# Unsplit expert tiles of a PEER layer over four PSUM banks instead of two, and 40 of them instead of 36

## The chip, the cores and the metric

The kernel runs on one core of one Trainium2 chip. The metric is the device time of one execution in microseconds (us). TensorE (PE) multiplies matrices and writes to PSUM, VectorE (DVE) and ScalarE (ACT) work elementwise, GpSimd (POOL) does so too and issues gathers from DRAM, and SyncE (SP) issues the plain loads and stores. Each engine takes its instructions strictly in the order in which they were written for it. "PEld" is the load of the stationary operand into TensorE.

## The reference

One layer for a prompt of 256 tokens and 8 samples of 16 tokens (128 tokens): modulated norm, a wide projection, an RWKV branch and a sparse attention branch, a mix of the two, and then PEER, a layer that picks experts by product keys. The change lies in PEER:

```python
def block(hb):                                   # 128 tokens, D = 1024
    q = (hb @ w_pq).reshape(PEER_BLOCK, PEER_HEADS, 2, PEER_DHALF)
    s = jnp.einsum('nhpd,hpkd->nhpk', q, peer_keys).astype(jnp.float32)
    s1, i1 = lax.top_k(s[:, :, 0], PEER_TOPK)
    s2, i2 = lax.top_k(s[:, :, 1], PEER_TOPK)
    cand = (s1[..., :, None] + s2[..., None, :]).reshape(PEER_BLOCK, PEER_HEADS, PEER_TOPK * PEER_TOPK)
    ...
    sc, j = lax.top_k(cand, PEER_TOPK)
    e = jnp.take_along_axis(cidx, j, axis=-1)
    g = jax.nn.softmax(sc, axis=-1)
    act = jax.nn.gelu(jnp.einsum('nhkd,nd->nhk', peer_u[e], hb).astype(jnp.float32))
    return jnp.einsum('nhk,nhkd->nd', (g * act).astype(hb.dtype), peer_v[e])
```

There are 8 heads, 16 picks for each and 16,384 experts, and all data is 32-bit floating point.

## The kernel before

Everything up to PEER takes the first half of the span. PEER treats the two groups of tokens in two ways.

- The 128 sample tokens go the sparse way (`peer_sparse`): for each of 128 picks, one gather by POOL brings a row of `peer_u` and `peer_v` for each token into a ring of three buffers (`raw`, L1573). DVE forms the dot product with the token (L1580), ACT applies gelu and the weight (L1581, L1582), and DVE adds the weighted row to `acc` (L1586). One such round is called a pull here. A gather waits until the `acc` of three pulls earlier has freed its buffer.
- The 256 prompt tokens go the dense way: all 16,384 experts are computed, as 128 u tiles of 128 experts (`dense_u`), the result is multiplied by a weight that is zero for experts not picked (`weights`), and 128 v tiles (`dense_v`) sum up the output.

A u tile loads 128 x 1024 numbers into one of four buffers `w`, multiplies them with the tokens into a PSUM tile of 128 x 256, and ACT writes the gelu of that to `G` (L1489), which frees the PSUM tile. The first `N1` u tiles are unsplit: 8 products of plain 32-bit operands with `h2f`, each of which the compiler turns into two matrix instructions, 16 for a tile. From tile `N1` on, a tile is split: ACT rounds it to a high part `wh` (L230), DVE subtracts for a low part `wl` (L234), and TensorE does 24 products with the split tokens `h2h` and `h2l`. So an unsplit tile asks nothing of DVE and one short gelu of ACT, and a split tile asks 128 x 1024 of each besides.

The unsplit tiles stand in the code beside the selection (`peer_select`, which finds the picks on DVE for the three groups of 128 tokens). After them the memory of `h2f` and of the selection is given up and taken over by the buffers of the split tiles and of `weights`: the first `wh` waits for the last read of `h2f`, and the first work of `weights` on DVE (L1424) waits for the last transposes of the selection's result `pix` on TensorE (L1384). Tiles `N1` to 75 follow, then `weights` with 31 more split u tiles among it, then the v tiles with the last 21 u tiles.

PSUM has eight banks, shared out by `PSB` under five names: `mm` 2 (projections, later `weights`), `fx` 2, `bx` 1, `dx` 2, `cp` 1. A u tile takes the name `u`, which stands for `fx`; so the u tiles go round two banks.

A pull is asked for after every u tile from tile `S0` = 30 on, at half a pull for each. But the order of the instructions of every engine is not the order of the code: a scheduler with a model of durations sets it, and moves pulls and u tiles forward to where it sees an engine free. No order is changed on the chip.

```python
PSB = {"mm": 2, "fx": 2, "bx": 1, "dx": 2, "cp": 1}
ALIAS = {"ix": "cp", "cs": "bx", "u": "fx"}
```

Of the kernel before, what the change touches and what calls it, by code (L numbers as in the profile page):

```python
# [176 lines left out]
ORDER = "GGIggggR1R23DMMMGRMRDMRGMGMRMDGMMRRMGDMMMGGGMGGM"  # L177


N1, NW, NA, NB = 36, 76, 8, 24  # L180
SR, UR = (0.5, 0.5, 0.62), 0.5
S0, PH = 30, 4
OFF = [j for j in range(NW, 128) if (j - NW + 1) * NB // (128 - NW) > (j - NW) * NB // (128 - NW)]
# [12 lines left out]
class K:  # L196
# [1274 lines left out]
    def dense_u(self, j):  # L1471

        nc = self.nc
        u = self.expert(self.I["puT"][j].rearrange("p k e -> p (k e)"))
        p = self.ps([128, 256], tag="u")
        if j < N1:
            u = u.rearrange("p (k e) -> p k e", k=8)
            for k in range(8):
                self.mm(p, u[:, k], self.h2f[:, k], start=(k == 0), stop=(k == 7))
        else:  # L1480
            uh, ul = (x.rearrange("p (k e) -> p k e", k=8) for x in self.split(u, UENG[j % len(UENG)]))
            hi, lo = self.h2p
            for k in range(8):
                self.mm(p, uh[:, k], hi[:, k], start=(k == 0), stop=False)
                self.mm(p, uh[:, k], lo[:, k], start=False, stop=False)
                self.mm(p, ul[:, k], hi[:, k], start=False, stop=(k == 7))
        off = j in OFF
        g = self.G[:, j] if j < NW else self.t([128, 256], tag="gO" if off else "gA", bufs=2 if off else NA, pool=self.late)
        nc.scalar.activation(g, p, AF.Gelu_apprx_tanh)  # L1489
        if off:  # L1490
            nc.sync.dma_start(self.Ad[OFF.index(j)], g)
        return g
# [262 lines left out]
```

## Time and profile before

| | us |
|---|---|
| median of three executions | 1782.42 |
| the three | 1770.41, 1782.42, 1785.15 |
| the profiled execution | 1775.45 |
| its span, first to last instruction | 1773.6 |
| mean granted TensorE clock in it | 0.977 of full speed |

All times below are from the profiled execution, counted from its first instruction. PEER's dense part has three stages there: the selection with the unsplit tiles beside it (some 880 to 1027), the split tiles and `weights` (1027 to 1300), and the v tiles (1300 to the end). A row of the timeline gives start, duration, engine, line, operation, the tile written and the tiles read, how many instructions were merged into the row, and in brackets the idle time before it and what ended that. Durations overlap on TensorE and, by a little, on DVE, so that what an instruction costs in a full queue is the distance from its start to the next start.

### The profile page before, as it was taken

How to read it: one execution, taken by the hardware profiler on the slowest of the kernel's cores; microseconds unless marked ns; L12 is line 12 of the kernel's file. 1: busy time of each engine (PE TensorE's matmuls, PEld its weight loads, DVE VectorE, ACT ScalarE, POOL GpSimd, SP SyncE). 2: the span in 40 equal slices, each digit the busy share in tenths (PEclk: the TensorE clock that was granted, in tenths of full speed). 3: DMA queues.
4: the chain of work that ended last, by engine and by line, in shares of the span. 5: the costliest groups of instructions: out<-in, count | busy, mean ns of one | idle time of the engine just before them, and what ended most of it. 6: DMA issues, size and time to landing. Idle time of an engine off the chain costs nothing. (4 is left out here: it accounts for less than half of the span.)

```text
span 1773.6 us, 33200 instructions
## 1 busy us (share of the span) xinstructions
PE 1682.0 (95%) x12424; PEld 1409.4 (79%) x12424; DVE 1358.9 (77%) x2911; ACT 751.1 (42%) x1670; POOL 537.9 (30%) x616
## 2 busy tenths in 40 slices
PE   6999899999999999999999989999999999999988
PEld 4888788777888877999878789999976667767766
DVE  4448778777867766556999998899847777778787
ACT  4533343334342333334323365577843433433344
POOL 2433243333333320034033222422233224223331
PEclk8999899999999999999999999999999999999999
DMA  8543662455365356755488989987569999999995
GB/s 307 156 125 98 184 192 70 144 166 168 94 205 149 101 198 188 247 188 187 129 336 320 370 310 383 378 316 261 178 236 362 347 349 379 354 364 385 340 366 218
DMA packets 172537, 436.71 MB, mean 246 GB/s; under 512 B 46036, under 2 KB 86100, under 8 KB 155992
## 3 DMA queue, kind: packets, MB, share of 16 engines
q1 hardware_dynamic: 153944, 300.36, 50.4%
q0 software_dynamic: 18432, 134.23, 19.8%
q8 instruction: 98, 1.61, 0.4%
q14 instruction: 63, 0.52, 0.1%
HBM read 403.23 MB, written 31.30 MB: 245 GB/s over the span
## 5 line engine op out<-in xcount | busy, mean ns | idle before, releaser
L234 DVE TENSOR_TENSOR wl<-w,wh 128x1024 fp32r<-128x1024 f32 (+1 forms) x280 | 351.1, 1261 | 106.7 <-ACT wh L230 69.8
L230 ACT ACTIVATE wh<-w 128x1024 fp32r<-128x1024 f32 (+1 forms) x288 | 300.3, 1051 | 162.0 <-PE mm L226 75.0
L1573 POOL DMA_INDIRECT raw<-in_puv,pe x128 | 172.8, 1350 | 430.1 <-PE dx L226 137.1
L226 PE MATMUL fx<-h2h,wh 128*128 128x256 f32 x736 | 210.6, 286 | 4.6 <-ACT wh L230 4.2
L226 PE MATMUL fx<-h2h,wl 128*128 128x256 f32 x736 | 208.3, 284 | 5.9 <-DVE wl L234 5.7
L226 PE MATMUL fx<-h2l,wh 128*128 128x256 f32 x736 | 206.5, 281 | 0.0
L1586 DVE SCALAR_TENSOR_TENSOR acc<-raw,dots,acc 128x1024 f32<-128x1024 f32 x127 | 167.4, 1318 | 15.1 <-ACT dots L1582 15.0
L1580 DVE SCALAR_TENSOR_TENSOR raw<-raw,sh 128x1024 f32<-128x1024 f32 x128 | 159.5, 1246 | 15.2 <-DMA raw<-in_puv,pe 15.1
L226 PEld LDWEIGHTS fx<-h2h,wh 128*128 128x128 f32 x736 | 139.6, 190 | 10.0 <-ACT wh L230 7.5
L226 PEld LDWEIGHTS fx<-h2h,wl 128*128 128x128 f32 x736 | 139.2, 189 | 9.0 <-DVE wl L234 8.3
L226 PEld LDWEIGHTS fx<-h2l,wh 128*128 128x128 f32 x736 | 139.7, 190 | 1.8 <-issue 1.4
L226 PE MATMUL fx<-h2f,w 128*128 128x256 f32 x576 | 129.5, 385 | 7.2 <-ACT G L1489 7.2
L226 PEld LDWEIGHTS fx<-h2f,w 128*128 128x128 f32 x576 | 109.4, 192 | 25.4 <-ACT G L1489 10.0
L226 PE MATMUL mm<-LTh,wh 128*128 128x384 f32 (+2 forms) x352 | 123.4, 351 | 1.8 <-ACT wh L230 1.0
L226 PE MATMUL mm<-LTl,wh 128*128 128x384 f32 (+2 forms) x352 | 123.0, 349 | 1.3 <-POOL LTl L488 1.3
L226 PE MATMUL mm<-LTh,wl 128*128 128x384 f32 (+2 forms) x352 | 122.3, 347 | 0.0
L226 PE MATMUL mm<-wh,LTh 128*128 128x256 f32 x336 | 100.4, 299 | 2.9 <-ACT qx L888 2.9
L226 PE MATMUL mm<-wl,LTh 128*128 128x256 f32 x336 | 99.6, 297 | 0.0
L226 PE MATMUL mm<-wh,LTl 128*128 128x256 f32 x336 | 98.9, 294 | 0.0
L1581 ACT ACTIVATE dots<-dots 128x1 f32<-128x1 f32 x128 | 25.6, 200 | 154.9 <-DVE raw L1580 154.4
L226 PEld LDWEIGHTS mm<-LTh,wh 128*128 128x128 f32 (+2 forms) x352 | 66.4, 189 | 7.6 <-issue 2.8
L226 PEld LDWEIGHTS mm<-wh,LTh 128*128 128x128 f32 x336 | 65.5, 195 | 5.5 <-ACT qx L888 3.1
(576 smaller groups left out, 4167.0 us busy)
## 6 DMA issues: line engine op xcount, KB each, us to landing
w<-in_puT SPq DMA_DIRECT2D x128, 512.0 KB
w<-in_pv SPq DMA_DIRECT2D x128, 512.0 KB
w<-in_w_in SPq DMA_DIRECT2D x70, 512.0 KB
w<-in_w_ada SPq DMA_DIRECT2D x48, 512.0 KB
cKT<-in_cKT SPq DMA_DIRECT2D x32, 256.0 KB
cV<-in_cV SPq DMA_DIRECT2D x32, 256.0 KB
w<-in_w_pq SPq DMA_DIRECT2D x16, 512.0 KB
d<-wst SPq DMA_DIRECT2D x8, 832.0 KB
```

What stands on the lines that cost most here:

```text
L226: return self.nc.tensor.matmul(out, l, r, start=start, stop=stop, skip_group_check=True, **kw)
L230: self.nc.scalar.activation(hi, src, AF.Copy)
L234: (self.nc.vector if eng == "v" else self.nc.gpsimd).tensor_tensor(lo, src, hi, op=OP.subtract)
L1573: d = nc.gpsimd.indirect_dma_start(out=bass.AP(tensor=u.tensor, offset=u.offset, ap=[u.ap[0], [1, 2048]]), out_offset=None, in_=self.I["puv"],
L1580: nc.vector.scalar_tensor_tensor(u, u, 1.0, h2, op0=OP.mult, op1=OP.mult, accum_out=dot)
L1581: nc.scalar.activation(dot, dot, AF.Gelu_apprx_tanh)
L1586: nc.vector.scalar_tensor_tensor(acc, v, dot, acc, op0=OP.mult, op1=OP.add)
```

## The change

```diff
-N1, NW, NA, NB = 36, 76, 8, 24
+N1, NW, NA, NB = 40, 76, 8, 24
@@ dense_u(self, j)
-        p = self.ps([128, 256], tag="u")
+        p = self.ps([128, 256], tag="mm" if j < N1 and j % 2 else "u")
```

Unsplit tiles with an odd number now go to the two `mm` banks, the others stay in the two `fx` banks, so that four banks hold u tiles while the selection runs; the split tiles keep two. Tiles 36 to 39 (counted from 0), which were split, become unsplit. Elsewhere the code is the same; the scheduler's order around the border of the two stages is not. Three places follow; in them `fx` and `mm` read from `h2f` are unsplit tiles, `fx` read from `h2h`, `h2l` are split ones, and the products of `oh` are those of `weights`.

TensorE at the border, before: the last two unsplit tiles, the three transposes of the selection's result (`dx`), and the first split tiles.

```order
L226 MATMUL fx_11740<-h2f_9800,w_11738 128x256 x8
L1384 MATMUL dx_11297<-cfirst,pix_11259 128x128
L226 MATMUL fx_11752<-h2f_9800,w_11750 128x256 x8
L1384 MATMUL dx_11297<-cfirst,pix_11259 128x128
L1384 MATMUL dx_11297<-cfirst,pg_2219_11290 128x128
L226 MATMUL fx_11783<-h2h_11769,wh_11784 128x256
L226 MATMUL fx_11783<-h2l_11770,wh_11784 128x256
L226 MATMUL fx_11815<-h2h_11769,wh_11816 128x256
L226 MATMUL fx_11815<-h2l_11770,wh_11816 128x256
L226 MATMUL fx_11783<-h2h_11769,wl_11785 128x256
```

TensorE at the same border in the changed kernel, from the 37th unsplit tile on.

```order
L226 MATMUL fx_11771<-h2f_9800,w_11769 128x256 x8
L226 MATMUL mm_11783<-h2f_9800,w_11781 128x256 x5
L1384 MATMUL dx_11297<-cfirst,pix_11259 128x128
L1384 MATMUL dx_11297<-cfirst,pg_2219_11290 128x128
L226 MATMUL mm_11783<-h2f_9800,w_11781 128x256 x3
L226 MATMUL fx_11802<-h2f_9800,w_11800 128x256 x8
L226 MATMUL mm_11814<-h2f_9800,w_11812 128x256 x8
L226 MATMUL mm_13141<-oh_13138 128x128 x4
L226 MATMUL bx_13155<-oh_13148 128x128 x4
L226 MATMUL mm_13207<-oh_13204 128x128 x4
L226 MATMUL fx_11845<-h2h_11831,wh_11846 128x256
L226 MATMUL fx_11845<-h2l_11832,wh_11846 128x256
```

The last transposes now stand inside the 38th unsplit tile, with 2 3/8 unsplit tiles behind them, and three groups of `weights` stand ahead of the first split tile.

DVE behind the last reduction of the selection (L1365), before: one `acc`, the first small work of `weights`, and the first `wl`.

```order
L1365 TENSOR_REDUCE pix_11259<-poh_11283 128x64
L1586 SCALAR_TENSOR_TENSOR acc_11699<-raw_13410,dots_13412,acc_11699 128x1024
L1424 CAST wA_13206<-pT_2172_11065 128x128
L1448 TENSOR_TENSOR oh_13218<-pT_2172_11065,dx_13204 128x512
L1425 TENSOR_SCALAR wA_13206<-wA_13206 128x128
L234 TENSOR_TENSOR wl_11785<-w_11781,wh_11784 128x1024
L1426 CAST wab_13207<-wA_13206 128x128
```

DVE at the same place in the changed kernel.

```order
L1365 TENSOR_REDUCE pix_11259<-poh_11283 128x64
L1586 SCALAR_TENSOR_TENSOR acc_11699<-raw_13330,dots_13332,acc_11699 128x1024
L1580 SCALAR_TENSOR_TENSOR raw_13397,dots_13399<-raw_13397,sh_2290_11697 128x1024
L1586 SCALAR_TENSOR_TENSOR acc_11699<-raw_13397,dots_13399,acc_11699 128x1024
L1424 CAST wA_13126<-pT_2172_11065 128x128
L1448 TENSOR_TENSOR oh_13138<-pT_2172_11065,dx_13124 128x512
L1425 TENSOR_SCALAR wA_13126<-wA_13126 128x128
L1426 CAST wab_13127<-wA_13126 128x128
L1580 SCALAR_TENSOR_TENSOR raw_13470,dots_13472<-raw_13470,sh_2290_11697 128x1024
```

A whole pull, the 27th, now stands ahead of `weights`, and no `wl`.

DVE a few rows on, before: the rows up to the `wl` of the 41st u tile (the fifth split one).

```order
L1580 SCALAR_TENSOR_TENSOR raw_13550,dots_13552<-raw_13550,sh_2290_11697 128x1024
L234 TENSOR_TENSOR wl_11888<-w_11884,wh_11887 128x1024
L1401 TENSOR_TENSOR oh_13218<-wA_13213,wB_13214 128x512
L1401 TENSOR_TENSOR oh_13228<-wA_13213,wB_13214 128x512
L1401 TENSOR_TENSOR oh_13284<-wA_13213,wB_13214 128x512
L1448 TENSOR_TENSOR oh_13284<-pT_2172_11065,dx_13204 128x512
L1580 SCALAR_TENSOR_TENSOR raw_13616,dots_13618<-raw_13616,sh_2290_11697 128x1024
L1586 SCALAR_TENSOR_TENSOR acc_11699<-raw_13550,dots_13552,acc_11699 128x1024
L234 TENSOR_TENSOR wl_11927<-w_11923,wh_11926 128x1024
```

DVE in the changed kernel, right behind the rows above: up to the `wl` of the 41st u tile (here the first split one).

```order
L1427 SCALAR_TENSOR_TENSOR wab_13127<-wab_13127,pT_2172_11065 128x128
L1437 TENSOR_TENSOR wA_13133<-wab_13127,clate 128x256
L1440 TENSOR_TENSOR wB_13134<-wab_13127,clate 128x512
L1439 TENSOR_TENSOR wA_13133<-wA_13133,pT_2172_11065 128x256
L1586 SCALAR_TENSOR_TENSOR acc_11699<-raw_13470,dots_13472,acc_11699 128x1024
L1401 TENSOR_TENSOR oh_13138<-wA_13133,wB_13134 128x512
L1401 TENSOR_TENSOR oh_13148<-wA_13133,wB_13134 128x512
L1401 TENSOR_TENSOR oh_13204<-wA_13133,wB_13134 128x512
L1448 TENSOR_TENSOR oh_13204<-pT_2172_11065,dx_13124 128x512
L1580 SCALAR_TENSOR_TENSOR raw_13536,dots_13538<-raw_13536,sh_2290_11697 128x1024
L1401 TENSOR_TENSOR oh_13214<-wA_13133,wB_13134 128x512
L234 TENSOR_TENSOR wl_11847<-w_11843,wh_11846 128x1024
```

In both kernels DVE has by then done 29 dot products of pulls and 28 additions to `acc`; the changed one has one more product of L1401 behind it and four `wl` fewer. Up to the first multiplication into `G` (L1413) the order before has 48 dot products, 48 additions and 41 `wl`, that of the changed kernel 50, 49 and 37; from the middle of `weights` on both stand at 58 pulls. On ACT the gelus of tiles 37 to 40 now stand ahead of the first `wh`, among the pulls. The order of the loads on SP and that of the v stage on all engines are nearly the same in both.

## The prediction

> **What bounds the kernel now.** First the totals of the page and the busy times of four stretches (start and end, length, then busy us and count of PE, PEld, DVE, ACT, POOL, then the granted TensorE clock, the DMA engines' share and GB/s).
>
> ```profile
> PE 1682.0 (95%) x12424; PEld 1409.4 (79%) x12424; DVE 1358.9 (77%) x2911; ACT 751.1 (42%) x1670; POOL 537.9 (30%) x616
> 880.00:1021.00 141.00, 133.83 (x623) 114.03 (x619) 139.25 (x545) 44.07 (x111) 39.99 (x33) 0.99 0.90 332
> 1027.00:1148.00 121.00, 119.75 (x1020) 118.67 (x1021) 110.72 (x129) 69.48 (x148) 36.87 (x23) 0.98 0.95 363
> 1148.00:1300.00 152.00, 143.43 (x1196) 140.50 (x1195) 141.13 (x199) 119.41 (x315) 42.41 (x39) 0.98 0.68 239
> 1300.00:1774.00 474.00, 449.04 (x1909) 319.65 (x1907) 355.50 (x422) 182.82 (x368) 146.01 (x125) 1.00 0.92 343
> 1296.00:1300.00 4.00, 3.52 (x25) 2.87 (x24) 2.64 (x5) 3.63 (x12) 1.66 (x2) 1.00 0.00 0
> ```
>
> The selection (first stretch) belongs to DVE: 139.25 of 141 us. The split tiles behind it (second) belong to TensorE, 119.75 of 121, with 10 us free on DVE. In `weights` (third) both are at 93 to 94%. The v tiles (fourth) live on loads, which begin only when `weights` ends: the last row shows DMA empty just before. So what ends earlier ahead of 1300 moves the v stage forward whole.
>
> Next the groups of instructions in the first stretch (busy us and mean ns, then idle time before), the queue of the loads, and TensorE's timeline.
>
> ```profile
> L226 PE MATMUL fx<-h2f,w 128*128 128x256 f32 x576 | 129.5, 385 | 7.2 <-ACT G L1489 7.2
> L1586 DVE SCALAR_TENSOR_TENSOR acc<-raw,dots,acc 128x1024 f32<-128x1024 f32 x24 | 31.0, 1290 | 0.0
> L1580 DVE SCALAR_TENSOR_TENSOR raw<-raw,sh 128x1024 f32<-128x1024 f32 x25 | 30.7, 1228 | 1.1 <-DMA raw<-in_puv,pe 1.1
> SPq L1463 <- PE fx L226: 124.2, 35, 7.5
> 890.71 29.58 PE L226 MATMUL fx<-h2f,w 128*128 128x256 f32 x128 [2.48 <-ACT G L1489]
> 921.32 14.08 PE L226 MATMUL fx<-h2f,w 128*128 128x256 f32 x64 [1.03 <-ACT G L1489]
> 1017.59 3.62 PE L226 MATMUL fx<-h2f,w 128*128 128x256 f32 x16
> 1024.79 0.47 PE L1384 MATMUL dx<-cfirst,pix 128*128 128x128 f32 x1 [3.58 <-DVE pix L1365]
> 1027.01 0.58 PE L226 MATMUL fx<-h2h,wh 128*128 128x256 f32 x1 [1.52 <-ACT wh L230]
> 1033.02 0.28 PE L226 MATMUL fx<-h2h,wl 128*128 128x256 f32 x1
> 1035.74 0.28 PE L226 MATMUL fx<-h2h,wl 128*128 128x256 f32 x1
> 1043.43 0.28 PE L226 MATMUL fx<-h2h,wl 128*128 128x256 f32 x1
> ```
>
> TensorE waits for a gelu to free one of the two banks, 7.2 us in all and 2.48 at most; then, at the border, 3.58 us for the selection's last reduction and 1.52 for the first `wh`. The loads wait for TensorE to give buffers back (SP's row), so they follow its pace.
>
> **The change, part by part.** *The price of a tile.* In the row at 921.32, 64 instructions take 14.08 us; with the last one's 0.38 us tail taken off, 63 steps of 0.2175, so an unsplit tile costs 16 steps, 3.48 us. Between the rows at 1033.02 and 1035.74 lie 24 steps, one split tile: 2.72 us. Four tiles moved therefore take 4 x 2.72 = 10.9 us out of the second stretch, where TensorE bounds, and put 4 x 3.48 = 13.9 us into the first, where DVE bounds. DVE loses four `wl`, ACT four `wh`; the gelus and loads stay.
>
> *The four banks.* With two more banks TensorE may run two tiles, 7 us, further ahead of the gelus. The longest wait was 2.48, so I cost the waits at between 0 and all of 7.2 us removed and take nearly all. What is late next is the selection: TensorE's transposes of `pix` stand in the order with 2 3/8 unsplit tiles behind them. Before, the 36th tile ended at 1021.2 (row at 1017.59). With all waits gone it ends at 1014.0, the transposes are reached 1.6 tiles (5.6 us) later at 1019.6, and TensorE waits there for `pix` until 1024.8, as before. With none gone they are reached at 1026.8. Behind them come 2.4 x 3.48 = 8.3 us, so the 40th tile ends between 1033.4 and 1035.5. The removed waits come back as one wait for `pix`; the banks by themselves are worth 0 to 2 us at that point. The extra tiles' loads are hidden by SP's waiting for TensorE; if that cover went, one would cost what DMA is late.
>
> *The border on DVE.* This decides, since `wl` of the first split tile now stands far behind on DVE, and three groups of `weights` stand ahead of that tile on TensorE. The rows with which I rebuild DVE's order are these, with two gathers, the pull that waited for the second of them, and the end of one pull's ACT part.
>
> ```profile
> 1023.68 1.06 DVE L1365 TENSOR_REDUCE pix<-poh 128x64 f32<-128x256 bf16 x2
> 1024.66 1.27 DVE L1586 SCALAR_TENSOR_TENSOR acc<-raw,dots,acc 128x1024 f32<-128x1024 f32 x1
> 1025.85 0.22 DVE L1424 CAST wA<-pT 128x128 uint32<-128x128 f32 x1
> 1025.99 0.68 DVE L1448 TENSOR_TENSOR oh<-pT,dx 128x512 f32<-128x512 f32 x1
> 1026.59 0.22 DVE L1425 TENSOR_SCALAR wA<-wA 128x128 uint32<-128x128 uint32 x1
> 1028.13 0.22 DVE L1426 CAST wab<-wA 128x128 bf16<-128x128 uint32 x1
> 1028.26 1.22 DVE L1580 SCALAR_TENSOR_TENSOR raw<-raw,sh 128x1024 f32<-128x1024 f32 x1
> 1029.41 1.22 DVE L234 TENSOR_TENSOR wl<-w,wh 128x1024 fp32r<-128x1024 f32 x1
> 1030.54 0.29 DVE L1427 SCALAR_TENSOR_TENSOR wab<-wab,pT 128x128 bf16<-128x128 bf16 x1
> 1030.75 0.42 DVE L1437 TENSOR_TENSOR wA<-wab,clate 128x256 f32<-128x256 bf16 x1
> 1033.41 0.69 DVE L1440 TENSOR_TENSOR wB<-wab,clate 128x512 bf16<-128x512 bf16 x1
> 1034.02 0.42 DVE L1439 TENSOR_TENSOR wA<-wA,pT 128x256 f32<-128x256 f32 x1
> 1036.63 1.90 DVE L1401 TENSOR_TENSOR oh<-wA,wB 128x512 f32<-128x512 f32 x3
> 1041.38 2.36 DVE L234 TENSOR_TENSOR wl<-w,wh 128x1024 fp32r<-128x1024 f32 x2
> 1021.81 2.35 POOL L1573 DMA_INDIRECT raw<-in_puv,pe  x1 [5.41 <-DVE acc L1586]
> 1041.74 1.68 POOL L1573 DMA_INDIRECT raw<-in_puv,pe  x1 [5.35 <-DVE acc L1586]
> 1051.04 1.23 DVE L1580 SCALAR_TENSOR_TENSOR raw<-raw,sh 128x1024 f32<-128x1024 f32 x1 [0.28 <-DMA raw<-in_puv,pe]
> 1029.76 0.30 ACT L1582 ACTIVATE dots<-dots,pg 128x1 f32<-128x1 f32 x1
> ```
>
> Start to start, `acc` costs 1.19, a dot product 1.15, `wl` 1.13, a product of L1401 or L1448 0.60. DVE's work up to the last reduction is the same rows in the same order, so it ends at 1024.66 again. Then: `acc` to 1025.85; the 27th dot to 1027.0; its weight comes from ACT 0.6 later (a dot ending at 1029.41 had its ACT part done at 1030.06), so `acc` runs 1027.6 to 1028.8; L1424, L1448, L1425, L1426 take 1.1, to 1029.9. The 28th pull's gather is that of 1021.81, as before; the one of 1041.74 landed at 1051.04, 9.3 later, so the 28th dot starts at 1031.1 and ends at 1032.3. L1427 to L1439 take 1.5, `acc` 1.2 (to 1035.0), three L1401 1.8, L1448 0.6, the 29th dot 1.15, another L1401 0.6: the first `wl` starts at about 1039.1 and ends at 1040.2.
>
> TensorE's first group of `weights` needs the first L1401, 1035.6, when the 40th tile has just ended; the three groups fill it until about 1038, and the third product of the first split tile, the 41st u tile, runs at 1040.3. Before, that product ran at 1043.43, with 0.2 us more done for the next tile. The gain is 1043.4 - 0.2 - 1040.3 = 2.9 us. DVE tells the same: `wl` of this tile was at 1041.38, now 1039.1 with 0.6 more work done, again 2.9. The saving of 10.9 us on TensorE shrinks to that because DVE, not TensorE, releases the 41st tile.
>
> *Behind the border.* Tiles 41 to 76 are unchanged. Up to the first multiplication into `G`, 1.5 more pulls stand on DVE, 1.5 x (1.23 + 1.29) = 3.8 us, within its 10 free us: cost nothing, and if that cover were gone, 3.8. They are then missing from the third stretch, where DVE and TensorE share the bound: worth 0 to 3.8, and since TensorE is as full as DVE there, I take 1.6. The v stage keeps its order: 0.
>
> Sum: 2.9 + 1.6 = 4.5 us less. On the profiled execution that is 1775.45 - 4.5 = 1771.0. The four executions shown (1770.41, 1775.45, 1782.42, 1785.15) have a mean of 1778.4; the profiled one is 7 below the median of the three. I put the forecast against the mean: 1774.
>
> **A rule weighed.** These are the clocks behind the border's waits.
>
> ```profile
> 1026.00:1028.00 2.00, 0.84 (x3) 0.55 (x3) 1.82 (x4) 2.00 (x4) 0.94 (x1) 0.50 0.96 377
> 1032.00:1034.00 2.00, 2.00 (x20) 2.00 (x19) 2.00 (x3) 1.46 (x3) 0.23 (x1) 1.00 1.02 371
> ```
>
> After 3.58 and 1.52 us of idling the clock is at half, and whole again 5 us on. A wait of 5 us for `pix` would do the same to the last unsplit tiles, some 2 us on the 40th tile's end: 1035.4 instead of 1033.4, still inside my bounds. The Trainium skill, page "TensorE: Matmul & The Clock Gate", Part 1 on the clock gate, says that an idle window of about 3.4 us halves the clock until about 3.4 us of sustained work; the trace agrees. By that rule an early TensorE wins nothing from the banks, and the sum stays at 4.5 with less in reserve, which speaks for the slower rival.
>
> **The rivals.** *More of it arrives.* If pulls or `weights` rows on DVE run closer than I strung them, the gain is bounded by the 10.9 us of TensorE; some 9.5 gives 1766 on the profiled base. Against it: DVE has saved only 4 x 1.13 = 4.5 us itself.
>
> *Nothing arrives.* The third stretch absorbs the 2.9 us, since its waits among ACT, DVE and TensorE fall differently: 1775.5. For it: no engine is above 94% there, so none passes on a lead surely.
>
> *Slower.* The first `wh` on ACT waits for the gelu of the 40th tile, and so for that tile's end; `wl` follows 1.4 us later. From an end of 1037.7 on, TensorE instead of DVE holds `wl` back, us for us; from some 1040.6 the change loses. It would take a late load or a half clock on top of kept gelu waits (DMA share is 0.90 to 0.95 there). 1044.5 would cost 4: 1779.5.
>
> **How the numbers follow.** The forecast (a gain of 1.5 to 8) has a chance of 0.50, nothing 0.20, slower 0.18, more 0.12. No case reaches 1% (17.8 us), which is about what a measurement of this kernel can tell from no change; beyond it lie only spread (the three executions differ by 0.8%) and what I have not seen: faster 0.06, same 0.91, slower 0.03. The range goes from the lowest execution less TensorE's whole saving, 1770.4 - 10.9 = 1759.5, to the highest plus the slower rival's 4, 1789.
>
> **What would show it.** 40 unsplit tiles at 3.48 us; gelu waits near zero and a wait of some 5 us for `pix` in the 38th tile; the first `wl` at about 1039; `weights` ending some 4.5 us earlier; the v stage as long as before. A first `wl` behind 1042, or an end of `weights` unmoved, proves me wrong.

## The result, and the profile after

| | us |
|---|---|
| before, median of 8 executions | 1778.18 (1770.41 to 1785.15) |
| after, median of 8 executions | 1764.09 (1759.49 to 1766.88) |
| ratio | 0.9924, 95% interval 0.9905 to 0.9943 |
| profiled execution after, and its span | 1759.49, 1757.7 |

The change makes the kernel 0.8% faster: less than 1%, but surely more than nothing. In microseconds it is 14 where 4.5 were forecast. One execution among all runs below, 2069.86 us at a granted clock of 0.745 instead of some 0.98, is left out of the ratios (it belongs to the run with the subtraction done twice for the first four split tiles). The totals of the page tell little of where they come from:

```profile
PE 1679.5 (96%) x12392; PEld 1410.2 (80%) x12392; DVE 1353.6 (77%) x2907; ACT 747.5 (43%) x1666; POOL 550.5 (31%) x616
```

So the trace is cut by events that both kernels have: the first unsplit u product; the end of the last reduction of the selection (L1365); the first product of the 41st u tile with `wl` (at 1043.43 in the prediction's rows); DVE's first multiplication into `G` (L1413); the first v product; the end. Here are the three stretches behind the selection, first before (start and end, length, busy us and count of PE, PEld, DVE, ACT, POOL, granted clock, DMA share, GB/s):

```profile
1024.80:1043.40 18.60, 16.93 (x126) 16.23 (x127) 18.42 (x27) 12.76 (x28) 5.22 (x3) 0.83 0.81 285
1043.40:1147.90 104.50, 103.41 (x897) 102.61 (x896) 94.22 (x107) 58.20 (x123) 32.35 (x21) 1.00 0.97 374
1147.90:1299.00 151.10, 142.53 (x1195) 140.08 (x1193) 141.22 (x200) 118.77 (x314) 41.96 (x39) 0.98 0.69 241
```

The same three after:

```profile
1020.80:1035.30 14.50, 13.09 (x74) 11.46 (x72) 13.87 (x25) 8.15 (x23) 4.96 (x3) 1.00 1.01 372
1035.30:1144.40 109.10, 105.63 (x892) 103.89 (x893) 97.46 (x109) 59.15 (x126) 36.95 (x21) 1.00 0.96 370
1144.40:1288.50 144.10, 140.28 (x1196) 138.09 (x1195) 138.18 (x195) 117.14 (x311) 43.90 (x37) 1.00 0.69 243
```

The border gained 4.1 us (18.6 to 14.5; 19.3 and 19.1 in two more profiles with 36 tiles). The stretch behind it gave all of that back (104.5 to 109.1). Then the last stretch, with most of `weights`, gained 7.0, of which the prediction had taken 1.6. Everything below is worked out around these three numbers.

Single executions scatter by several us, so each cut was taken in every profiled execution of the study. "Ahead" is the time up to the first unsplit product, where the orders are alike; "selection" goes from there to the end of L1365; "border + behind" joins the first two stretches above.

| kernel | ahead | selection | border + behind | last stretch | v stage |
|---|---|---|---|---|---|
| before | 880.4 | 144.4 | 123.1 | 151.1 | 474.6 |
| before, again | 880.3 | 143.7 | 123.7 | 152.2 | 473.3 |
| four banks, 36 tiles | 882.0 | 144.4 | 124.8 | 150.7 | 474.3 |
| after (four banks, 40 tiles) | 876.3 | 144.5 | 123.6 | 144.1 | 469.2 |
| after, again | 886.2 | 144.0 | 121.5 | 144.0 | 469.5 |
| after, a third time | 878.8 | 143.7 | 122.5 | 145.4 | 472.9 |
| two banks, 40 tiles | 875.8 | 143.9 | 123.3 | 144.0 | 475.8 |
| two banks, 40 tiles, again | 877.3 | 144.1 | 121.1 | 144.2 | 471.6 |
| four banks, 38 tiles | 880.0 | 144.3 | 121.0 | 150.2 | 467.7 |
| four banks, 44 tiles | 885.1 | 144.6 | 124.4 | 142.3 | 475.5 |

Border, behind it and last stretch together take 274.2, 275.9 and 275.5 with 36 tiles, and 267.7, 265.5 and 267.9 in the changed kernel: a mean gain of 8.2 us. The selection doesn't move. The mean of "ahead" is 880.9 with 36 tiles and 880.4 in the changed kernel, so the 4 us by which the first profile after leads there is scatter. The v stage is shorter in the mean by 3.6 us (474.1 to 470.5), but 40 tiles on two banks, with the same order there, gave 475.8 and 471.6; that part stays open.

On TensorE the border looks like this after (start, duration, and in brackets the idle time before and what ended it):

```profile
942.90 0.45 PE L1384 MATMUL dx<-cfirst,pix 128*128 128x128 f32 x1 [4.87 <-DVE pix L1365]
...
1012.98 0.30 PE L1384 MATMUL dx<-cfirst,pix 128*128 128x128 f32 x1 [1.95 <-DVE pix L1365]
...
1022.24 0.27 PE L1384 MATMUL dx<-cfirst,pix 128*128 128x128 f32 x1
...
1027.21 3.62 PE L226 MATMUL mm<-h2f,w 128*128 128x256 f32 x16
1030.72 1.13 PE L226 MATMUL mm<-oh 128*128 128x128 f32 x8
...
1035.31 0.39 PE L226 MATMUL fx<-h2h,wl 128*128 128x256 f32 x1 [1.42 <-DVE wl L234]
```

No wait for a gelu is left among the unsplit tiles. TensorE waits instead for the selection, at the transposes of `pix` for earlier groups of tokens (4.87 and 1.95), and then no longer at the last ones, inside the 38th tile. The 40th tile ends at about 1030.8, and `weights` follows without a gap. The last product shown is the third of the 41st u tile; DVE's `wl` released it.

### The profile page after: what moved, and what is told of

Its sections match the earlier page's. It is cut to its first block, busy times and chain, and to the rows that moved or that the text cites. A ratio compares the mean times of both kernels' runs of the same rounds, so it can differ in the third digit from the quotient of the medians.

```text
span 1757.7 us, 33129 instructions
## 1 busy us (share of the span) xinstructions
PE 1679.5 (96%) x12392; PEld 1410.2 (80%) x12392; DVE 1353.6 (77%) x2907; ACT 747.5 (43%) x1666; POOL 550.5 (31%) x616
## 4 chain that ended last, share of the span: by engine, by line
PE 55%; DVE 19%; DMA 11%; issue 8%; ACT 3%; POOL 2%; SPq 1%; DVEq 0%; POOLq 0%; ACTq 0%
PE mm L226 21%; PE fx L226 10%; PE dx L226 10%; PE cp L226 6%; PE bx L226 6%; DMA raw<-in_puv,pe 3%; DVE wl L234 3%; DVE raw L1580 2%; DVE acc L1586 2%; DMA w<-in_puT 2%; DMA w<-in_pv 2%; ACT wh L230 1%; DMA w<-in_w_in 1%; DVE TX L698 1%; DMA NL<-d 1%
## 5 line engine op out<-in xcount | busy, mean ns | idle before, releaser
L234 DVE TENSOR_TENSOR wl<-w,wh 128x1024 fp32r<-128x1024 f32 (+1 forms) x276 | 345.8, 1260 | 109.0 <-ACT wh L230 71.3
L226 PE MATMUL fx<-h2h,wl 128*128 128x256 f32 x704 | 200.1, 285 | 8.2 <-DVE wl L234 8.0
L226 PE MATMUL fx<-h2h,wh 128*128 128x256 f32 x704 | 200.6, 285 | 1.4 <-ACT wh L230 1.1
L226 PE MATMUL fx<-h2l,wh 128*128 128x256 f32 x704 | 197.4, 281 | 0.0
L226 PEld LDWEIGHTS fx<-h2h,wl 128*128 128x128 f32 x704 | 132.7, 189 | 12.3 <-DVE wl L234 11.5
L226 PEld LDWEIGHTS fx<-h2h,wh 128*128 128x128 f32 x704 | 132.6, 188 | 6.4 <-ACT wh L230 3.6
L226 PEld LDWEIGHTS fx<-h2l,wh 128*128 128x128 f32 x704 | 132.9, 189 | 1.6 <-issue 1.1
L226 PE MATMUL mm<-LTl,wh 128*128 128x384 f32 (+2 forms) x352 | 123.1, 350 | 0.9 <-POOL LTl L488 0.9
L226 PE MATMUL mm<-h2f,w 128*128 128x256 f32 x448 | 104.0, 385 | 0.0
L226 PEld LDWEIGHTS mm<-h2f,w 128*128 128x128 f32 x448 | 85.0, 192 | 12.2 <-issue 0.2
L226 PE MATMUL fx<-h2f,w 128*128 128x256 f32 x320 | 73.8, 383 | 0.0
```

Source lines behind the costliest of these rows:

```text
L226: return self.nc.tensor.matmul(out, l, r, start=start, stop=stop, skip_group_check=True, **kw)
L234: (self.nc.vector if eng == "v" else self.nc.gpsimd).tensor_tensor(lo, src, hi, op=OP.subtract)
```

## The experiments

### The two halves of the change, each alone

Four banks and still 36 tiles:

```diff
-        p = self.ps([128, 256], tag="u")
+        p = self.ps([128, 256], tag="mm" if j < N1 and j % 2 else "u")
```

> Four banks for the unsplit tiles, still 36 of them; the order of every engine is that of before. Theory A (the tiles moved make the gain, the banks only give room for them): the waits of TensorE for a gelu go from 7 us to under 2, come back as a wait of some 5 us for pix at the border, the selection stays 144 us long, and the time is within 3 us of before (ratio 0.998 to 1.002). Rival B (the banks make the gain): stretch A or the border is shorter by 5 us or more, ratio 0.997 or less.

Measured: ratio 1.0006 (0.9989 to 1.0022). Its list of TensorE's waits from the first unsplit product to the border (waiter, awaited, us in all, times, longest) is a single line:

```profile
PE dx L1384 <- DVE pix L1365: 10.7, 3, 4.9
```

The 7.2 us of waits for gelus are gone and have come back as waits for the selection, which grew from 3.6 us to 10.7: in all TensorE waits as long as before. They lie at three of its transposes and not, as expected, at the border alone. The banks alone are worth nothing that shows.

The other half, 40 tiles on two banks, is the changed kernel with the second line of the diff undone:

> 40 unsplit tiles with two banks; the order of every engine is that of the changed kernel. Theory A: the 40th tile ends some 2 to 5 us later than in the changed kernel, the first wl is delayed by 0 to 4 us, and most of the gain of 14 us is still there, ratio 0.993 to 0.996. Rival B: without the banks the 40 tiles gain nothing, ratio 0.998 or more.

Measured: ratio 0.9944 (0.9924 to 0.9964). The 40th tile ended 10.5 us behind the selection instead of 10.0, where 2 to 5 us had been expected: all that the banks win there is 0.5 us. The first split product with `wl` came at 17.0 instead of 14.5, but that was not the banks. DVE's `wl` released it in both kernels, and DVE was late because in this execution the 28th pull had to wait for its gather:

```profile
1027.44 1.23 DVE L1580 SCALAR_TENSOR_TENSOR raw<-raw,sh 128x1024 f32<-128x1024 f32 x1 [2.29 <-DMA raw<-in_puv,pe]
...
1036.69 0.39 PE L226 MATMUL fx<-h2h,wl 128*128 128x256 f32 x1 [1.44 <-DVE wl L234]
```

At the first multiplication into `G` nothing is left of the delay (123.3 against 123.6).

For the scatter between executions, both kernels were profiled once more:

> The kernel before once more, for a second profile: how far each stretch differs between executions of the same kernel. If the selection's start (880.4), the stretch of weights (151.1) and the v stage (474.6) come back within 1 us, the differences to the changed kernel (876.3, 144.1, 469.2) are its own; if they scatter by 4 us or more, the start and the v stage of the first two profiles tell nothing.

> The changed kernel once more, for a second profile. Expected from the first: 123.6 us from the end of the selection to the first multiplication into G, 144.1 of weights, both within 1 us; if the v stage's gain of 5.4 us and the start's of 4.1 us are scatter, they come out elsewhere.

They took 1774.94 and 1766.97 us; their stages are in the table. The last stretch repeats within 1.1 us (1.5 with the third profile after), and so the 7 us there are no accident of one profile. The part ahead of it repeats less well than expected in the changed kernel: 123.6 and then 121.5.

Since the v stages of the two kernels with 40 tiles differed by 6 us, both ran again side by side:

> The changed kernel once more, beside the one with 40 tiles on two banks. If the banks are worth nothing (theory), its ratio is that of the other within 0.002, and its v stage (first v product to the end) lies at 469 to 476 like that of the other. If the v stage gains from the four banks or the order around them (rival), its v stage is again at 469 to 470, the other's again at 475 to 476, and the ratios differ by some 0.003.

> 40 unsplit tiles on two banks, a second time. Theory (banks worth nothing): ratio as that of the changed kernel within 0.002. Rival (the v stage is longer without the two extra banks): v stage 475 to 476, ratio some 0.003 higher than that of the changed kernel. The first split product with wl again 2 to 2.5 us later behind the selection's end than with four banks, and that lead again gone at the first multiplication into G.

Measured: ratio 0.9924 (0.9899 to 0.9949) with four banks and 0.9942 (0.9916 to 0.9968) with two, medians 1766.01 and 1766.23 of 12 executions each. The v stages were 472.9 and 471.6: the gap of 6 us did not repeat. Nor did the delay of the first split product with `wl`, of which 2 to 2.5 us had been expected again: it came 15.2 us behind the selection, with 0.45 us of waiting for the gather. Over all executions of the study, the mean is 1764.6 for four banks (21) and 1766.8 for two (18); the difference is 2.1 us, with an interval of 2.8 to either side. So most of the gain belongs to the 40 tiles: alone they show some 10 of the 14 us. A share of the banks is neither shown nor excluded.

### More and fewer tiles

```diff
-N1, NW, NA, NB = 40, 76, 8, 24
+N1, NW, NA, NB = 44, 76, 8, 24
```

> 44 unsplit tiles over four banks: four more tiles than the changed kernel leave the split stage. Theory A (the gain is DVE's: four wl fewer on the engine that bounds): again 4.5 us or more on top of the changed kernel, ratio to before 0.990 or less, as long as TensorE's four more tiles (13.9 us behind the selection) are covered by the groups of weights and pulls on DVE. Rival B (TensorE at the border bounds now): the first wl product moves from 14.5 us behind the selection to 22 or later, nothing more is gained, ratio 0.992 to 0.997.

Measured: ratio 0.9945 (0.9928 to 0.9962), as rival B had it. The first split product with `wl` comes 30.1 us behind the selection, twice as late as with 40 tiles, because the last unsplit tiles now hold up TensorE there; at that product it no longer waits for `wl`. The end of the last one, and that product:

```profile
1053.39 3.62 PE L226 MATMUL mm<-h2f,w 128*128 128x256 f32 x16
...
1059.81 0.38 PE L226 MATMUL fx<-h2h,wl 128*128 128x256 f32 x1
```

The last stretch gains another 2 us (142.3) and the border with what is behind it loses them (124.4): together 266.7, as with 40. Then with 38:

> The changed kernel with 38 unsplit tiles instead of 40 (four banks). Up to the first multiplication into G its order has 49 dot products and 48 additions, one dot product more than before (50 and 49 with 40 tiles), and two groups of weights instead of seven stand behind the last u tile. Theory (DVE work taken out of the last stretch plus the waits at its tail): border gain about half of 3.8, last stretch 151.1 less 1.2 less up to 4 for the tail = 146 to 150, ratio 0.995 to 0.998. Rival (the gain grows with the number of tiles on TensorE, 2.72 us each): half the gain, ratio 0.996, with the last stretch unchanged at 151 and the stretch ahead of it 3 us shorter.

Measured: ratio 0.9942 (0.9916 to 0.9967). The sum of the three stretches is 271.2 in its one profile, half way between the means of 275.2 and 267.0, so the stages speak for a gain that grows with the tiles up to 40; the times of whole executions don't separate 38 from 40. And the gain lies where the rival had put it, ahead of the last stretch (121.0), and that stretch itself is almost unchanged:

```profile
1145.34:1295.50 150.16, 142.59 (x1208) 140.48 (x1209) 141.55 (x198) 119.44 (x314) 45.02 (x38) 0.99 0.68 239
```

Its order has one dot product more than the kernel before had by the first multiplication into `G`, with 40 tiles it is two and an addition: how much moves from one stretch to the other is the scheduler's choice. DVE's work there was not less than before (141.55 us against 141.22), and its idle time, the length less the busy time, hardly (8.6 against 9.9). The 4 us that the theory took from waits at the tail did not come.

### Is DVE the bound?

In the changed kernel the subtraction for `wl` was done twice for the first four split tiles, which gives DVE back the 4.5 us that the change had taken from it; what is computed stays the same. Up to the first multiplication into `G` the order has as many pulls as that of the changed kernel.

```diff
-            uh, ul = (x.rearrange("p (k e) -> p k e", k=8) for x in self.split(u, UENG[j % len(UENG)]))
+            uh, ul = self.split(u, UENG[j % len(UENG)])
+            if j < N1 + 4:
+                nc.vector.tensor_tensor(ul, u, uh, op=OP.subtract)
+            uh, ul = (x.rearrange("p (k e) -> p k e", k=8) for x in (uh, ul))
```

> The changed kernel with the subtraction for wl done twice for the first four split tiles: the same results, four more instructions of 1.13 us on DVE, nothing else. This gives DVE back the time that the change took from it; TensorE keeps its 40 unsplit tiles. Theory A (DVE bounds the split stage and weights): 4.5 us are lost in the two stretches, or up to 7 with the tail of weights, ratio to before 0.995 to 0.998. Rival B (TensorE's 10.9 us are the gain): nothing is lost, ratio 0.991 to 0.994.

Measured: ratio 0.9975 (0.9954 to 0.9996). The row from the end of the selection to the first multiplication into `G`:

```profile
1021.80:1151.30 129.50, 120.87 (x962) 116.34 (x960) 116.36 (x139) 68.27 (x149) 38.89 (x24) 0.99 0.93 354
```

DVE is busy 5.0 us longer than in the changed kernel (13.87 + 97.46 = 111.3), and the stretch takes 129.5 instead of 121.5 to 123.6: it loses all of the added work and a little more, though DVE is still idle for 13 us of it. For work that stands ahead of a `wl` which TensorE wants, that idle time is no slack: TensorE waits 3.2 us for the second subtractions themselves. With the last stretch (145.8) the sum is 275.3, as before the change (275.2): in this profile nothing of the stages' gain is left, though TensorE kept its 40 unsplit tiles. Of the time of whole executions some 4 us of gain remain.

The same question for the last stretch: the doubled subtraction moved to tiles inside it.

```diff
-            if j < N1 + 4:
+            if j in (78, 82, 86, 90):
```

> The changed kernel with DVE's subtraction for wl done twice for the u tiles 78, 82, 86 and 90 (the same result). On TensorE the order through weights is that of the changed kernel, seven groups behind the last u tile included; on DVE it carries 36 instead of 33 wl between the first multiplication into G and the end of weights, 3 x 1.13 = 3.4 us more, which is what the two dot products and one addition that the change took out of this stretch had cost (3.5). Theory (the gain in that stretch, 151.1 to 144.1 us, is half DVE work taken out, 3.5, and half waits of DVE that the better order of the tail removed, 4): the stretch takes about 147.5, the ratio to the kernel before is about 0.9945. Rival A (work alone; DVE's waits only reflect it): 150 to 151, ratio 0.996 or more. Rival B (the tail's order alone, DVE has room): 144 to 145, ratio 0.9925 as the changed kernel.

Measured: ratio 0.9965 (0.9943 to 0.9987). The last stretch, as a row, and two of DVE's groups in it:

```profile
1148.43:1298.20 149.77, 142.77 (x1196) 140.57 (x1195) 143.45 (x198) 116.75 (x311) 43.41 (x37) 0.98 0.68 234
```

```profile
L1440 DVE TENSOR_TENSOR wB<-wab,clate 128x512 bf16<-128x512 bf16 x6 | 6.8, 1128 | 0.0
L1483 DVE TENSOR_TENSOR wl<-w,wh 128x1024 fp32r<-128x1024 f32 x3 | 3.6, 1210 | 0.0
```

The three extra `wl` of this stretch took 3.6 us, and the stretch 5.7 more than the profile after (5.3 more than the mean of the three). DVE's busy time grew by 5.3: the further 1.7 are instructions that took longer than usual, like those of L1440 (1128 ns in the mean; 683 in the changed kernel), of which the three slow ones stand beside multiplications into `G` on POOL. DVE's idle time stayed low, 6.3 us where the changed kernel has 5.9 and the kernel before 9.9. The theory had 147.5 and the rival of DVE's work alone 150 to 151: the time is nearly the rival's, but the waits that it wanted to see again did not return. Work on DVE costs its full price here, and more.

### Two ways that might have helped the kernel before

If four `wl` less on DVE are what counts, they could go to POOL, in the kernel before with its 36 tiles:

```diff
-            uh, ul = (x.rearrange("p (k e) -> p k e", k=8) for x in self.split(u, UENG[j % len(UENG)]))
+            uh, ul = (x.rearrange("p (k e) -> p k e", k=8) for x in self.split(u, 'g' if j < N1 + 4 else 'v'))
```

> The kernel before (36 unsplit tiles, two banks) with the wl of the four tiles 36 to 39 made by POOL instead of DVE: DVE gets its 4.5 us, TensorE and ACT get nothing. Theory A: half or more of the gain, ratio 0.993 to 0.997, if POOL, at some 3 us each, is not itself late with them. Rival B: no gain, ratio 0.998 or more.

Measured: ratio 0.9989 (0.9968 to 1.001). The border and what is behind it grew to 132.7 us, the last stretch fell to 145.9, with DVE busy 137.6 us there. Two rows of DVE's timeline there, and two of POOL's:

```profile
1025.57 7.45 DVE L1426 CAST wab<-wA 128x128 bf16<-128x128 uint32 x1
...
1041.22 3.75 DVE L1586 SCALAR_TENSOR_TENSOR acc<-raw,dots,acc 128x1024 f32<-128x1024 f32 x1 [0.60 <-ACT dots L1582]
```

```profile
1025.89 7.04 POOL L234 TENSOR_TENSOR wl<-w,wh 128x1024 fp32r<-128x1024 f32 x3
...
1041.47 2.42 POOL L234 TENSOR_TENSOR wl<-w,wh 128x1024 fp32r<-128x1024 f32 x1
```

A cast that takes 0.22 us (L1426 in the prediction's rows) takes 7.45 and ends with POOL's three subtractions; an `acc` of 1.28 takes 3.75 and ends 1.1 us behind POOL's fourth, as if it had begun its work only then. By the records each of the two began 0.3 us ahead of POOL's and stood all the same. DVE lost 7.2 + 2.5 = 9.7 us to work that had been taken off it, and the stretch is 9 longer. So this run is no test of whether less DVE work helps; it shows that POOL is no place for it. The Trainium skill, page "SBUF — State Buffer", section on the two separate sides, says that VectorE and GpSimd share one pair of ports, held by one of them for a whole instruction while the other is blocked, where VectorE's instruction runs in a two-port mode or has two inputs in SBUF and GpSimd's reads SBUF. The trace agrees for the `acc`, which has two such inputs and lost 2.5 us to 2.42 of POOL; in which mode the cast ran it doesn't show, and the cast stood for three instructions and not for one.

In the last stretch before, the last groups of `weights` stood alone, TensorE waited among them and the clock fell:

```profile
1288.00:1292.00 4.00, 4.00 (x19) 4.00 (x20) 3.42 (x6) 1.26 (x3) 0.42 (x1) 0.50 0.90 327
```

To see whether that half clock cost the 7 us, four products that nobody reads were put behind each of the last twelve groups in the kernel before:

```diff
+            if i == 2 and n >= 80:
+                x = self.ps([128, 128], tag="dx")
+                for j in range(4):
+                    self.mm(x, oh[:, 1, j], oh[:, 0, j])
```

> The kernel before with four products more, into a spare bank and read by nobody, behind each of the last 12 groups of weights. They keep TensorE busy where it waited for DVE and ACT at the end of weights and its clock fell to half. If the half clock there cost the kernel before some 3 us, the clock stays at full, and the last 20 us of weights shrink by 1 to 3; if DVE and ACT set that pace anyway, the stretch of weights stays at 151 us or grows by up to 5.

Measured: ratio 1.0014 (0.9994 to 1.0035), and the last stretch is longer, not shorter:

```profile
1148.10:1303.70 155.60, 149.57 (x1281) 147.12 (x1281) 143.07 (x200) 119.92 (x315) 41.94 (x39) 1.00 0.67 235
```

The clock is whole (1.00 against 0.98), TensorE is busy 7.0 us longer and the stretch takes 4.5 more. Raising the clock this way wins nothing that pays for the products. What the half clock costs by itself was not separated.

## Why the prediction was right and wrong

Its class, "same", and its range held, but both were wide enough for every case that it weighed; its time was 10 us too high. The gain of 14 us is three times the forecast and lies in the case "more", which had a chance of 0.12. The prediction took 1% for about what a measurement can tell from no change; the interval above reaches 0.2% to either side. Step by step:

**The price of a tile** was right: unsplit tiles start 3.45 us apart after (1023.76 and 1027.21), against 3.48.

**The four banks** were right in size and sign, wrong in place. They were costed at 0 to 2 us at the 40th tile and nothing at the end: they gave 0.5 at that tile, and alone 1.0006. The wait for `pix` came back at earlier transposes, not in the 38th tile. It does halve the clock, as the rule weighed there said: after the 4.87 us the granted clock is 0.50 for the next 6 us. The 40th tile ended 10.0 us behind the selection; 8.7 to 10.8 had been worked out.

**The border on DVE** was right in mechanism and 1.2 us too small: the first `wl` was put 14.4 us behind the selection, and it came at 13.3:

```profile
1019.72 1.08 DVE L1365 TENSOR_REDUCE pix<-poh 128x64 f32<-128x256 bf16 x2
...
1026.07 1.22 DVE L1580 SCALAR_TENSOR_TENSOR raw<-raw,sh 128x1024 f32<-128x1024 f32 x1
...
1034.03 1.23 DVE L234 TENSOR_TENSOR wl<-w,wh 128x1024 fp32r<-128x1024 f32 x1
```

The dot product at 1026.07 is that of the 28th pull. The prediction let it wait for its gather until 6.4 us behind the selection; it started 5.3 behind without any wait. That is the whole difference, and it changes from run to run: with two banks the same dot product did wait, 2.29 and 0.45 us. The gain at the 41st tile was 4.1 instead of 2.9.

**"Cost nothing"** is the step whose mechanism failed. The 1.5 pulls brought forward were to lie within 10 us of free time on DVE. DVE's groups behind the border (count, busy us and mean ns, idle before and what ended it), before:

```profile
L234 DVE TENSOR_TENSOR wl<-w,wh 128x1024 fp32r<-128x1024 f32 x36 | 43.8, 1222 | 7.1 <-ACT wh L230 6.8
L1586 DVE SCALAR_TENSOR_TENSOR acc<-raw,dots,acc 128x1024 f32<-128x1024 f32 x20 | 25.6, 1282 | 2.7 <-ACT dots L1582 2.7
L1580 DVE SCALAR_TENSOR_TENSOR raw<-raw,sh 128x1024 f32<-128x1024 f32 x19 | 23.2, 1221 | 0.5 <-DMA raw<-in_puv,pe 0.5
```

and after:

```profile
L234 DVE TENSOR_TENSOR wl<-w,wh 128x1024 fp32r<-128x1024 f32 x36 | 43.9, 1225 | 7.2 <-ACT wh L230 7.0
L1586 DVE SCALAR_TENSOR_TENSOR acc<-raw,dots,acc 128x1024 f32<-128x1024 f32 x21 | 27.0, 1284 | 0.6 <-ACT dots L1582 0.6
L1580 DVE SCALAR_TENSOR_TENSOR raw<-raw,sh 128x1024 f32<-128x1024 f32 x21 | 25.7, 1223 | 3.9 <-DMA raw<-in_puv,pe 3.9
```

The `wl` are as many, the pulls 1.5 more. Most of the idle time is DVE waiting for `wh`: it sits just ahead of a `wl` that TensorE wants next, and a pull can't be put there without making that `wl` late. TensorE shows it; here is its row before, and the one after:

```profile
L226 PE MATMUL fx<-h2h,wl 128*128 128x256 f32 x291 | 81.0, 279 | 0.9 <-DVE wl L234 0.7
```

```profile
L226 PE MATMUL fx<-h2h,wl 128*128 128x256 f32 x290 | 81.4, 282 | 4.3 <-DVE wl L234 4.3
```

Its waits for `wl` rose from 0.7 us to 4.3 (2.9 and 3.3 in the two repeats). The stretch took 109.1, 107.0 and 108.1 us against 104.5 (104.4 and 105.7 in the two other profiles with 36 tiles): 2.5 to 4.6 more than 104.5, around the 3.8 that the prediction had named for the case that the cover is gone. In the first profile a late gather (3.9) adds to it; in the repeats it is 1.2 and 2.2.

**The third stretch** was mis-sized: 1.6 us was taken, out of 0 to 3.8, and it gave 7.0 (6.8 between the means of three executions each). DVE's groups there, before:

```profile
L1401 DVE TENSOR_TENSOR oh<-wA,wB 128x512 f32<-128x512 f32 x55 | 39.7, 743 | 4.0 <-ACT oh L1453 2.0 <-ACT wst L1414 0.9 <-issue 0.6
...
L1413 DVE TENSOR_TENSOR G<-G,mm 128x304 f32<-128x304 f32 x32 | 14.7, 462 | 3.2 <-PE mm L226 3.2
```

and after:

```profile
L1401 DVE TENSOR_TENSOR oh<-wA,wB 128x512 f32<-128x512 f32 x55 | 41.3, 769 | 2.2 <-ACT wst L1414 1.3 <-PE cp L226 0.6 <-ACT oh L1453 0.2
...
L1413 DVE TENSOR_TENSOR G<-G,mm 128x304 f32<-128x304 f32 x31 | 14.2, 461 | 0.0
```

In DVE's account two parts make up the 7.0: DVE is busy 3.0 us less (141.22 to 138.18; two dot products and an addition are gone, 3.5), and idle 4.0 us less (9.9 to 5.9), above all in waits for TensorE's `mm` and for ACT's `oh`. All but 2.6 us of the waits before lay in the last 55 us of the stretch, where the order before left twelve groups of `weights` nearly alone and that of the changed kernel leaves seven. The prediction saw the first part and halved it, "since TensorE is as full as DVE there"; the doubled `wl` shows that DVE's work costs at least its full price, so it should have stood at 3.5. The second part it did not have at all: the diff of the order was read only around the border.

What took those waits away is not shown. The run that put the work back and kept the order of the tail speaks for the order: the idle time stayed at 6.3. Two others speak against the number of lone groups as the cause: with 38 tiles there are nine and DVE is idle 8.6 us, and with `wl` on POOL there are seven, as in the changed kernel, and it is idle 8.3. The work on DVE is the better shown part: the stretch lost 5.3 to 5.7 of its 7 us when 3.6 us of it were put back. Why the scheduler ordered it so was not tried.

**The v stage**, put at 0, was 3.6 us shorter in the mean of three profiles each, but one run with two banks and the same order there took 475.8, longer than any before. Whether it gained is open, and so are some 2 us between the 8.2 + 3.6 that the stages show and the 14 between the medians.

**The rivals.** The slower one didn't come: with 40 tiles the 40th ends 10.0 us behind the selection, and DVE, not TensorE, releases the 41st tile. With 44 its mechanism is there, and the gain stops growing. "Nothing arrives" rested on the third stretch absorbing the lead; the second did, and the third paid. What came is nearest to "more of it arrives" at 9.5, by another way than was written there. The bound of 10.9 us that it put on the gain is not refuted: the stages show 8.2, and the ratio's interval goes from 10 to 17 us.

## What to carry to other kernels

Idle time of an engine counts as cover only after asking where it lies: if it always ends with the input of something that the bounding engine wants next, added work can be paid in full. Work that an order moves from one stretch to another must be priced in both, and the whole order has to be compared, up to the end of the last stretch that it changes, not only where the diff points. Before DVE work is handed to POOL, look how long the neighbours on DVE take while POOL runs.

## What was unexpected of the hardware

Twice in the run with `wl` on POOL, work there held up DVE for as long as it ran, however short DVE's own instruction was: 3.75 us for an `acc` of 1.28 beside one subtraction, and 7.45 for a cast of 0.22, which did not get in between three subtractions that followed one another. In a small way it happens without that change too: in the last stretch of the kernel before, nine of DVE's `wl`, `acc` and `oh` instructions took 0.6 to 0.8 us longer than their like, each beside a POOL multiplication into `G` (L1413, 0.8 to 1.3 us).
